# A decoder layer's weight products: one load per block for two sums, reordered branch loads, and accumulating transfers in the output projection

## Chip, cores, metric

One core of one Trainium2 chip. The metric is device time of one execution in microseconds (us). TensorE's granted clock is one of two levels, 1.2 and 2.4 GHz; the profile shows it as 0.5 and 1.

## What is computed

One decoder layer on 512 tokens of width 2048, in float32. Cut to what matters:

```
proj = rms_norm(x) @ w_in                      # 2048 x 14928
y_a, y_b, y_m = three branches of proj, each 512 x 1024
merged = sigmoid(g_a) * (y_a @ w_branch_a) + sigmoid(g_b) * (y_b @ w_branch_b)
       + sigmoid(g_m) * (y_m @ w_branch_m)     # w_branch_*: 1024 x 2048
out = x + merged @ w_out                       # 2048 x 2048
```

Branch a is a gated MLP: a layer norm over v, a causal mix inside each chunk of 128 tokens, then a product with gelu(u) and silu(z).

## The kernel before

**Every product is three.** A float32 operand is split into a high and a low part: ScalarE (ACT) casts the high part and VectorE (DVE) subtracts it from the source (`split`, L136 and L137). `three` (L160 to L162) multiplies high by high, low by high and high by low. Weights pass through in blocks of 128 x 2 x 512 floats (512 KB, "one pair" of k tiles). The tile `raw` has four slots, the split parts `whi` and `wlo` three each. One pair in a block product is 12 matmuls.

**Strassen units.** Eight units of 1024 columns (v, z, m, m, b, b, a, a) of `w_in` go through `strassen` (L836): each needs seven block products instead of eight, A11, S1, S2, A12, S3, A22, N4, each of four pairs (48 matmuls). The weight operand of a product is either a block as loaded (`passing`, into `raw`) or a running sum of blocks kept in SBUF, `va` (tile `a`) and `vb` (tile `b`), to which DVE adds the next block (L847). S1 reads `va`, then adds block (1,1) to it (`b11_12`, L865); S2 reads `va`, loads block (1,1) again and adds it to `vb` (`b11_12_22`, L871); A12 reads block (1,0) as loaded and adds it to `va` (L877). `kept_as` stores each result to DRAM from the POOL (GpSimd) queue.

**The last unit** also starts loads for what follows, all from the POOL queue, as `last_unit` (L948) places them: after S1 the operand `ym` of branch m (four loads of 1 MB), after S3 `after_s3` (L935: a gate block, the factors of chunk 0, the layer norm's gain and bias), after A22 the operand `yb` of branch b (four of 1 MB).

**Branch stage** (L1078): for m, b, a and each of four column groups a product of 96 matmuls, whose result DVE multiplies by the gate (L1095) and adds up (L1097). `gating` (L963), a generator, does branch a's MLP for four chunks between the products; `pump` runs it a few steps per k tile against a credit, and each `yield` names what the step takes. Its input tiles come by `factors_load` (L928). `finish(made)` runs what is left of it before branch a's first product.

**Output projection**: `output_unit` (L1114) twice, 1024 columns of `w_out` each, in the order A11, S3, S1, S2, A12, A22, N4. All weight loads and the stores to `out` are issued on the SP (SyncE) queue, in one order; the blocks of `x` come into one tile, `score`, from POOL (`x_part`, L1127), and DVE adds them. The first of the two units runs while DVE still prepares its operands (`right_half`, `parts_of`).

**Order.** The build orders each engine's instructions by what it takes to be ready, not by the place in the code alone: an instruction can stand ahead of others that the code has earlier. On the chip each engine and queue then keeps that order.

Of the kernel before, what the change touches and what calls it, by code (L numbers as in the profile page):

```python
# [17 lines left out]
P = 128  # L18
# [41 lines left out]
def hybrid_block(ctx: ExitStack, tc: tile.TileContext, a, out):  # L60
# [41 lines left out]
    def submit(gen):  # L102
        tasks.append(gen)
        return gen
# [716 lines left out]

    pairs = range(0, 8, CK)

    def block_product(op, ps, operand, onto=False, budget=None):
        ah, al = op
        for k in pairs:
# [9 lines left out]
    def strassen(w, c0, finished, placing=None, after={}):  # L836
# [12 lines left out]
        def product(name, *args, **k):  # L849
            block_product(ops[name], *args, **k)  # L850
            if name in after:
                after[name]()

        va, vb = {}, {}

        def b11(k):
            va[k] = load(held("a"), 0, 0, k)
            parts = split_pair(va[k])
            vb[k] = load(held("b"), 0, 1, k)
            add(va[k], vb[k])  # L860
            if k == 8 - CK and placing:
                placing()
            return parts

        def b11_12(k):  # L865
            c = passing(1, 1, k)
            parts = split_pair(va[k])
            add(va[k], c)
            return parts

        def b11_12_22(k):  # L871
            c = passing(1, 1, k)
            parts = split_pair(va[k])
            add(vb[k], c)
            return parts

        def b21(k):  # L877
            c = passing(1, 0, k)
            parts = split_pair(c)
            add(va[k], c)  # L880
            return parts

        x = bank()
        product("A11", x, b11)
# [12 lines left out]
        x = bank()  # L897
        e3 = ev()
        V.tensor_tensor(e3, z, e1, op=OP.subtract)
        finished(1, 512, e3)  # L900
        product("A22", x, lambda k: split_pair(va[k]))
        V.tensor_tensor(e1, x, e1, op=OP.add)
        finished(1, 0, e1)
        product("N4", z, lambda k: split_pair(passing(1, 1, k)), onto=True)
        V.tensor_tensor(e2, z, e2, op=OP.subtract)
        finished(0, 512, e2)

    def kept_as(kept, func):
        def finished(th, col, t, psum=None):
# [6 lines left out]
    y_of, sgs, uvz, lnp = {}, {}, {}, []  # L916

    def y_load(name):
        y_of[name] = tuple(big16(f"y{name}{n}") for n in range(2))
        for n in range(2):  # L920
            for f in (0, 4):
                G.dma_start(y_of[name][n][:, f:f + 4, :].bitcast(F32), y_kept[name][n, :, f:f + 4, :])

    def gate_load(name, cg):
        sgs[name, cg] = big8([P, 4, T])
# [6 lines left out]

    wide8 = lambda: (big8([P, 2, 1024]), big8([P, 2, 1024]))

    def after_s3():  # L935
        gate_load("m", 0)
        factors_load(0, wide8)
        lnp.append(big8([P, 2, 1024]))
        for i, name in enumerate(("gain", "bias")):
            G.dma_start(lnp[0][:, i, :], a["gmlp_ln_" + name].partition_broadcast(P))  # L940
# [17 lines left out]
    y_of["a"] = tuple(pools["cpool"].tile([P, 8, T], F32R, tag=f"ya{n}", name=f"ya{n}") for n in range(2))  # L958
    odd8 = lambda tag="odd1": pools["cpool"].tile([P, 2, 1024], F32, tag=tag, name=tag)
    odd_two = lambda: (odd8("odd0"), odd8("odd1"))  # L960
    factors_load(1, odd_two)

    def gating():  # L963
        for c in range(NT):
            vo, uz = uvz.pop(c)
            u, v, o = uz[:, 0, :], vo[:, 0, :], vo[:, 1, :]
            bs = tiny.tile([P, 2, 6], F32, name="bn_s")
# [25 lines left out]
            for g2 in range(2):  # L993
# [84 lines left out]
    for name, cg in [(name, cg) for first in (0, 2) for name in "mba" for cg in (first, first + 1)]:  # L1078
        if (name, cg) not in sgs:
            gate_load(name, cg)  # L1080
        if name == "a" and made in tasks:
            finish(made)
        sg = sgs.pop((name, cg))
        ah, al = y_of[name]
        ps = [bank(), bank()]
        for k, hi, lo in chunks(a["w_branch_" + name], cg * 512, 512, 8):
# [24 lines left out]
    stage = opened(("ev", 4), ("hold", 4))  # L1111
    w_out = a["w_out"]

    def output_unit(c0, first):  # L1114
        wv = w_out.rearrange("(k p) c -> p k c", p=P)

        def load(to, kh, ch, k):
            SP.dma_start(to, wv[:, kh * 8 + k:kh * 8 + k + CK, c0 + ch * 512:c0 + ch * 512 + 512])
# [5 lines left out]
        def add(to, x):  # L1124
            V.tensor_tensor(to, to, x, op=OP.add)

        def x_part(th, col):  # L1127
            xr = score_all[:, :1024].rearrange("p (t c) -> p t c", c=512)
            G.dma_start(xr, a["x"].rearrange("(t p) c -> p t c", p=P)[:, 2 * th:2 * th + 2, c0 + col:c0 + col + 512])  # L1129
            return xr  # L1130

        def store(th, col, t, ts=slice(0, 2)):
            SP.dma_start(out.rearrange("(t p) c -> p t c", p=P)[:, 2 * th:2 * th + 2, c0 + col:c0 + col + 512][:, ts],
                         t[:, ts])
# [12 lines left out]

        def b11_12_22(k):
            add(va[k], passing(1, 1, k))
            return split_pair(va[k])  # L1150

        def b21(k):
            c = passing(1, 0, k)
            parts = split_pair(c)
            add(va[k], c)
            return parts

        bud = 1300 if first else None
# [6 lines left out]
        if first:  # L1165
            finish(submit(parts_of("S2")))
            n4_made = submit(parts_of("N4"))
# [5 lines left out]
        if first:  # L1173
            finish(n4_made)
        add_to = lambda o, p, q, op: V.tensor_tensor(o, p, q, op=op)  # L1175
        add_to(e1, y, e1, OP.add)
        e3 = ev()
        add_to(e3, z, e1, OP.subtract)
        add_to(e7, e1, e7, OP.subtract)
        xr = x_part(0, 0)  # L1180
        block_product(gops["A12"], x, b21, onto=True)
        add_to(xr, x, xr, OP.add)
        store(0, 0, xr)
        xr = x_part(1, 512)
        add_to(e3, e3, xr, OP.add)
        store(1, 512, e3)
        xr = x_part(1, 0)
        x = bank()
        add_to(xr, xr, e1, OP.add)
        block_product(gops["A22"], x, lambda k: split_pair(va[k]))  # L1190
        add_to(xr, x, xr, OP.add)
        store(1, 0, xr)
        xr = x_part(0, 512)
        add_to(e7, e7, xr, OP.subtract)
        block_product(gops["N4"], z, lambda k: split_pair(passing(1, 1, k)), onto=True)
        for t in range(2):
            add_to(e7[:, t], z[:, t], e7[:, t], OP.subtract)
            store(0, 512, e7, slice(t, t + 1))
# [41 lines left out]
```

## Time and profile before

| | us |
|---|---|
| median of 3 runs (1862.53 to 1866.06) | 1864.43 |
| the profiled execution, its own time | 1864.7 |
| its span, first to last instruction | 1863.0 |
| PE (TensorE) busy in it | 1811.2 |
| DVE busy | 1261.0 |
| ACT busy | 760.6 |

A row of the waits or of the timeline names the engine, the line, the operation and its tiles; "idle before <-X" says what ended the idle time. POOL and SP issue transfers. In the table of stretches each row is a stretch of the span, with busy time and instruction count of each engine, then the granted clock, the DMA engines' busy share and their rate.

### The profile page before, as it was taken

The numbers are of one execution on the slowest core, as the hardware profiler recorded it, in microseconds if no ns is written. First come the engines' busy times: TensorE is split into PE (matmuls) and PEld (weight loads), VectorE is DVE, ScalarE is ACT, GpSimd is POOL, SyncE is SP. The second block draws the span as 40 slices with busy tenths as digits, with TensorE's granted clock in tenths as the row PEclk, the third lists the DMA queues.
The fourth block names the chain that finished last, engine by engine and source line by source line (L and its number), as shares of the span: only waits on it lengthen the run. The fifth ranks groups of instructions, "written<-read, shape, count | busy, mean of one in ns | idle before, by whom it ended". The sixth has DMA issues, their size and how long they took to land. (4 is left out here: it accounts for less than half of the span.)

```text
span 1863.0 us, 21854 instructions
## 1 busy us (share of the span) xinstructions
PE 1811.2 (97%) x8426; PEld 1512.3 (81%) x8426; DVE 1261.0 (68%) x1667; ACT 760.6 (41%) x986; POOL 95.1 (5%) x155
## 2 busy tenths in 40 slices
PE   8999999999999999999999999999897999998997
PEld 6798899888888888888888888888786888886776
DVE  7787679665436466968678687786755543559685
ACT  4754442353334354444444444444351222225332
POOL 7000000000000000000000000000010000000000
PEclk9999999999999999999999999999998999998999
DMA  7744223333332424675665755756765544337673
GB/s 231 276 127 119 77 81 87 113 114 113 91 102 60 135 68 142 223 220 162 187 209 181 214 181 181 219 165 213 260 245 196 193 135 136 114 119 275 213 228 124
DMA packets 141720, 304.03 MB, mean 163 GB/s; under 512 B 10032, under 2 KB 16176, under 8 KB 139568
## 3 DMA queue, kind: packets, MB, share of 16 engines
q1 hardware_dynamic: 127200, 242.39, 41.9%
q0 software_dynamic: 14128, 60.23, 8.9%
q8 instruction: 66, 1.08, 0.2%
q14 instruction: 38, 0.31, 0.1%
q10 hardware_dynamic: 288, 0.02, 0.0%
HBM read 271.14 MB, written 31.46 MB: 162 GB/s over the span
## 5 line engine op out<-in xcount | busy, mean ns | idle before, releaser
L137 DVE TENSOR_TENSOR wlo<-raw,whi 128x1024 fp32r<-128x1024 f32 (+1 forms) x280 | 339.8, 1216 | 299.4 <-ACT whi L136 299.0
L136 ACT CAST whi<-raw 128x1024 fp32r<-128x1024 f32 (+1 forms) x280 | 288.5, 1031 | 566.3 <-PE xyz L162 275.8
L136 ACT CAST whi<-a 128x1024 fp32r<-128x1024 f32 x152 | 160.0, 1054 | 211.5 <-PE xyz L162 195.1
L161 PE MATMUL xyz<-wlo,hTh 128*128 128x512 f32 x576 | 225.2, 391 | 6.5 <-DVE wlo L137 6.5
L160 PE MATMUL xyz<-whi,hTh 128*128 128x512 f32 x576 | 224.9, 390 | 0.7 <-ACT b L752 0.7
L162 PE MATMUL xyz<-whi,hTl 128*128 128x512 f32 x576 | 225.0, 391 | 0.0
L137 DVE TENSOR_TENSOR wlo<-a,whi 128x1024 fp32r<-128x1024 f32 x152 | 184.7, 1221 | 48.8 <-ACT whi L136 48.3
L160 PE MATMUL acc<-whi,hTh 128*128 128x512 f32 (+1 forms) x544 | 203.5, 374 | 0.3 <-ACT b L639 0.3
L161 PE MATMUL acc<-wlo,hTh 128*128 128x512 f32 (+1 forms) x544 | 200.9, 369 | 0.0
L162 PE MATMUL acc<-whi,hTl 128*128 128x512 f32 (+1 forms) x544 | 200.6, 369 | 0.0
L161 PEld LDWEIGHTS xyz<-wlo,hTh 128*128 128x128 f32 x576 | 108.7, 189 | 29.6 <-DVE wlo L137 7.0
L160 PEld LDWEIGHTS xyz<-whi,hTh 128*128 128x128 f32 x576 | 108.7, 189 | 23.7 <-ACT b L752 1.1
L162 PEld LDWEIGHTS xyz<-whi,hTl 128*128 128x128 f32 x576 | 108.7, 189 | 22.6
L160 PEld LDWEIGHTS acc<-whi,hTh 128*128 128x128 f32 x544 | 102.2, 188 | 13.5 <-ACT b L639 0.7
L162 PEld LDWEIGHTS acc<-whi,hTl 128*128 128x128 f32 x544 | 102.1, 188 | 13.5
L161 PEld LDWEIGHTS acc<-wlo,hTh 128*128 128x128 f32 x544 | 102.3, 188 | 11.9
L185 PE MATMUL acc<-hTh,whi 128*128 128x512 f32 x256 | 100.1, 391 | 0.0
L186 PE MATMUL acc<-hTl,whi 128*128 128x512 f32 x256 | 99.7, 390 | 0.0
L187 PE MATMUL acc<-hTh,wlo 128*128 128x512 f32 x256 | 99.7, 389 | 0.0
L847 DVE TENSOR_TENSOR a<-a,raw 128x1024 f32<-128x1024 f32 x64 | 76.9, 1221 | 9.2 <-DMA raw<-w_in 8.7
L137 DVE TENSOR_TENSOR wlo<-b,whi 128x1024 fp32r<-128x1024 f32 x40 | 49.0, 1224 | 47.7 <-ACT whi L136 47.7
L136 ACT CAST whi<-b 128x1024 fp32r<-128x1024 f32 x40 | 42.0, 1050 | 47.0 <-PE xyz L162 42.2
(357 smaller groups left out, 3542.3 us busy)
## 6 DMA issues: line engine op xcount, KB each, us to landing
raw<-w_in SPq DMA_DIRECT2D x216, 512.0 KB, 3.6
raw<-w_out SPq DMA_DIRECT2D x48, 512.0 KB, 4.4
a<-w_in SPq DMA_DIRECT2D x32, 512.0 KB, 4.5
b<-w_in SPq DMA_DIRECT2D x32, 512.0 KB, 3.8
raw<-w_mem_kv SPq DMA_DIRECT2D x31, 512.0 KB, 4.7
raw<-w_in SPq DMA_DIRECT2D x24, 368.0 KB, 3.1
raw<-w_branch_m SPq DMA_DIRECT2D x16, 512.0 KB, 5.1
raw<-w_branch_b SPq DMA_DIRECT2D x16, 512.0 KB, 3.7
```

Source lines behind the costliest of these rows:

```text
L136: S.copy(hi, src)
L137: V.tensor_tensor(lo, src, hi.bitcast(F32), op=OP.subtract)
L160: PE.matmul(ps, lhsT=lh, rhs=rh, start=first, stop=False, **k)
L161: PE.matmul(ps, lhsT=lh, rhs=rl, start=False, stop=False, **k)
L162: PE.matmul(ps, lhsT=ll, rhs=rh, start=False, stop=last, **k)
L185: PE.matmul(ps[i][:m], lhsT=hi[:, f:f + m], rhs=ah[:, k, :], start=(k == 0), stop=False)
L186: PE.matmul(ps[i][:m], lhsT=hi[:, f:f + m], rhs=al[:, k, :], start=False, stop=False)
L187: PE.matmul(ps[i][:m], lhsT=lo[:, f:f + m], rhs=ah[:, k, :], start=False, stop=(k == ktiles - 1))
L847: V.tensor_tensor(to, to, x, op=OP.add)
```

## The change

1. `strassen`: block (1,1) is loaded once, in S1, and DVE adds it there to `va` and to `vb`; S2 neither loads nor adds.
2. `block_product` takes a list of calls and makes one after each pair. In the last unit the four loads of `ym` are asked for after S2's second and fourth pair and A12's first and second; the gate block, gain and bias, and chunk 0's factors after A22's first, second and third. `yb` is loaded at the start of branch m's second product. Chunk 1's and 3's factors are loaded inside `gating`, chunk 2's after chunk 1, with larger yields.
3. Output projection: `output_unit` is replaced by `first_output_unit` and, for the second half, by `strassen` with the same operands. In the first, the sums of S3 and S1 are made by a transfer from POOL that adds into the tile (`accum_op`) in place of a load and a DVE add. In both, `x` is added to three of four result blocks by such a transfer and they are stored from POOL; the last has `x` subtracted by DVE before N4, and is stored from SP.

```diff
         def product(name, *args, **k):
-            block_product(ops[name], *args, **k)
-            if name in after:
-                after[name]()
+            block_product(ops[name], *args, after=after.get(name, ()), **k)
...
         def b11_12(k):
             c = passing(1, 1, k)
             parts = split_pair(va[k])
             add(va[k], c)
+            add(vb[k], c)
             return parts
 
         def b11_12_22(k):
-            c = passing(1, 1, k)
-            parts = split_pair(va[k])
-            add(vb[k], c)
-            return parts
+            return split_pair(va[k])
...
+        if before_last:
+            before_last(e2)
         product("N4", z, lambda k: split_pair(passing(1, 1, k)), onto=True)
-        V.tensor_tensor(e2, z, e2, op=OP.subtract)
-        finished(0, 512, e2)
+        for t in (slice(0, 1), slice(1, 2)) if before_last else (slice(0, 2),):
+            V.tensor_tensor(e2[:, t], z[:, t], e2[:, t], op=OP.subtract)
+            finished(0, 512, e2, ts=t)
...
-    last_unit = {"S1": lambda: y_load("m"), "S3": after_s3, "A22": lambda: y_load("b")}
+    last_unit["S2"] = [lambda: None, first_of(ym), lambda: None, first_of(ym)]
+    last_unit["A22"] = [lambda: gate_load("m", 0), norm_load, lambda: factors_load(0, wide8)]
...
-    factors_load(1, odd_two)
...
         for c in range(NT):
+            if c + 1 < NT and c % 2 == 0:
+                factors_load(c + 1, odd_two)
...
-            if c + 2 < NT:
-                factors_load(c + 2, odd_two if c else wide8)
-                yield 3000
+            if c == 1:
+                factors_load(2, wide8)
+                yield 9000
+            elif c == 0:
+                yield 6000
...
+        if name == "m" and cg == 1:
+            for load in y_load("b"):
+                load()
...
+    def given_out(c0):
+        def finished(th, col, t, psum=None, ts=None):
+            o = ev() if t is None else t
+            if psum is not None:
+                S.copy(o, psum)
+            if ts is None:
+                G.dma_start(o, tiles_of(a["x"], th, c0 + col), accum_op=OP.add)
+                G.dma_start(tiles_of(out, th, c0 + col), o)
+            else:
+                SP.dma_start(tiles_of(out, th, c0 + col)[:, ts], o[:, ts])
+        return finished
+
+    def less_x(c0):
+        xr = score_all[:, :1024].rearrange("p (t c) -> p t c", c=512)
+        G.dma_start(xr, tiles_of(a["x"], 0, c0 + 512))
+        return lambda e2: V.tensor_tensor(e2, e2, xr, op=OP.subtract)
...
         def b12_22(k):
             vb[k] = load(held("b"), 0, 1, k)
-            add(vb[k], passing(1, 1, k))
+            G.dma_start(vb[k], block(1, 1, k), accum_op=OP.add)
             return split_pair(vb[k])
 
         def b11_12(k):
             va[k] = load(held("a"), 0, 0, k)
-            add(va[k], passing(0, 1, k))
+            G.dma_start(va[k], block(0, 1, k), accum_op=OP.add)
             return split_pair(va[k])
...
+        less = less_x(0)
         block_product(gops["A12"], x, b21, onto=True)
-        add_to(xr, x, xr, OP.add)
-        store(0, 0, xr)
+        finished(0, 0, None, x)
...
-    output_unit(0, True)
-    output_unit(1024, False)
+    first_output_unit()
+    strassen(w_out, 1024, given_out(1024), ops=gops, before_last=less_x(1024))
```

## Rows read from the trace of the kernel before

**Rows 1.** The page's part 1: busy time, share of the span, instructions.

```profile
PE 1811.2 (97%) x8426; PEld 1512.3 (81%) x8426; DVE 1261.0 (68%) x1667; ACT 760.6 (41%) x986; POOL 95.1 (5%) x155
```

**Rows 2.** Waits of PE: who, for what, us in total, times, longest.

```profile
PE xyz L161 <- DVE wlo L137: 18.0, 8, 6.5
PE xyz L160 <- DVE b L1095: 7.4, 2, 6.6
PE xyz L160 <- ACT whi L136: 5.5, 1, 5.5
```

**Rows 3.** Table of stretches, last unit of `w_in`: S2, then A12.

```profile
1319.60:1330.50 10.90, 10.90 (x50) 9.03 (x49) 8.40 (x8) 4.22 (x4) 2.15 (x4) 1.00 0.97 359
1330.50:1350.50 20.00, 13.47 (x50) 10.60 (x49) 10.66 (x11) 4.21 (x4) 1.29 (x2) 0.83 0.77 288
```

**Rows 4.** Timeline of POOL and DVE in the same two products.

```profile
1320.05 2.15 POOL L922 DMA_DIRECT2D ym<-y_m  x4 [17.69 <-PE xyz L162]
...
1337.92 1.23 DVE L847 TENSOR_TENSOR a<-a,raw 128x1024 f32<-128x1024 f32 x1 [4.05 <-DMA raw<-w_in]
```

**Rows 5.** Timeline of DVE and PE, start of S1 in the unit before the last.

```profile
1152.62 1.22 DVE L137 TENSOR_TENSOR wlo<-a,whi 128x1024 fp32r<-128x1024 f32 x1
...
1159.71 2.36 DVE L137 TENSOR_TENSOR wlo<-a,whi 128x1024 fp32r<-128x1024 f32 x2
...
1156.84 0.39 PE L161 MATMUL xyz<-wlo,hTh 128*128 128x512 f32 x1
```

**Rows 6.** Table of stretches, branch stage: first and second product of branch m.

```profile
1383.20:1405.50 22.30, 22.22 (x99) 18.03 (x97) 4.81 (x4) 6.34 (x6) 3.63 (x6) 1.00 0.93 335
1405.50:1443.80 38.30, 28.21 (x121) 22.59 (x120) 24.43 (x43) 6.50 (x9) 1.82 (x3) 0.82 0.48 166
```

**Rows 7.** Timeline of DVE and POOL in the branch stage.

```profile
1407.47 0.69 DVE L970 BATCH_NORM_STATS2 bn_s<-odd 128x6 f32<-128x512 f32 x1 [11.43 <-DMA odd<-kept_v]
...
1416.61 1.22 DVE L1095 TENSOR_TENSOR b<-b,xyz 128x1024 f32<-128x1024 f32 x1
...
1550.47 0.75 POOL L926 DMA_DIRECT2D b<-kept_b  x1 [2.02 <-PE aux L1014]
```

**Rows 8.** Table of stretches, output projection: first unit's S3, S1, N4; second's A11, S3; the end.

```profile
1690.00:1711.40 21.40, 14.39 (x49) 11.12 (x49) 20.80 (x20) 10.24 (x10) 0.71 (x1) 0.76 0.80 283
1711.40:1722.90 11.50, 11.13 (x49) 8.92 (x48) 11.32 (x11) 5.97 (x6) 0.00 (x0) 1.00 0.97 349
...
1755.60:1773.90 18.30, 13.73 (x49) 10.47 (x48) 9.35 (x8) 4.20 (x4) 1.43 (x2) 0.85 0.67 233
1773.90:1786.30 12.40, 11.88 (x50) 9.43 (x49) 9.02 (x9) 4.20 (x4) 0.71 (x1) 0.94 0.72 215
1786.30:1798.40 12.10, 11.10 (x49) 8.90 (x48) 10.29 (x10) 5.12 (x5) 0.00 (x0) 1.00 0.91 315
...
1853.40:1863.00 9.60, 0.03 (x1) 0.00 (x0) 2.51 (x3) 0.00 (x0) 0.25 (x1) 0.70 0.32 109
```

**Rows 9.** Timeline of DVE and SP, first output unit's S3.

```profile
1693.35 1.22 DVE L1125 TENSOR_TENSOR b<-b,raw 128x1024 f32<-128x1024 f32 x1
...
1683.60 2.27 SPq L1118 DMA_DIRECT2D b<-w_out  x4
1687.78 0.37 SPq L1118 DMA_DIRECT2D a<-w_out  x1
```

**Rows 10.** DMA issues: tile, queue, count, KB of one, median us to landing.

```profile
b<-kept_m POOLq DMA_DIRECT2D x4, 1024.0 KB, 8.7
...
score<-x POOLq DMA_DIRECT2D x8, 512.0 KB, 5.6
```

**Rows 11.** Timeline of DVE: first unit's N4, and the end of the kernel.

```profile
1765.30 1.23 DVE L1175 TENSOR_TENSOR score<-score,ev 128x1024 f32<-128x1024 f32 x1 [5.12 <-DMA score<-x]
...
1857.17 1.23 DVE L1175 TENSOR_TENSOR ev<-ev,score 128x1024 f32<-128x1024 f32 x1 [6.59 <-DMA score<-x]
1858.50 1.29 DVE L1175 TENSOR_TENSOR ev<-xyz,ev 128x512 f32<-128x512 f32 x2
```

More of the change, by code (lines that the diff above doesn't have):

```diff
@@ L822, in hybrid_block, with block_product @@
     pairs = range(0, 8, CK)
-    def block_product(op, ps, operand, onto=False, budget=None):
+    def block_product(op, ps, operand, onto=False, budget=None, after=()):
         ah, al = op
+        after = iter(after)
         for k in pairs:
@@ L834, in block_product, with strassen @@
                 pump(budget)
-    def strassen(w, c0, finished, placing=None, after={}):
+            next(after, lambda: None)()
+        for rest in after:
+            rest()
+    def strassen(w, c0, finished, placing=None, after={}, ops=ops, before_last=None):
         wv = w.rearrange("(k p) c -> p k c", p=P)
@@ L903, in strassen @@
         finished(1, 0, e1)
+        if before_last:
+            before_last(e2)
         product("N4", z, lambda k: split_pair(passing(1, 1, k)), onto=True)
-        V.tensor_tensor(e2, z, e2, op=OP.subtract)
-        finished(0, 512, e2)
+        for t in (slice(0, 1), slice(1, 2)) if before_last else (slice(0, 2),):
+            V.tensor_tensor(e2[:, t], z[:, t], e2[:, t], op=OP.subtract)
+            finished(0, 512, e2, ts=t)
     def kept_as(kept, func):
-        def finished(th, col, t, psum=None):
+        def finished(th, col, t, psum=None, ts=None):
             o = ev() if t is None else t
@@ L919, in y_load, with part @@
         y_of[name] = tuple(big16(f"y{name}{n}") for n in range(2))
-        for n in range(2):
-            for f in (0, 4):
-                G.dma_start(y_of[name][n][:, f:f + 4, :].bitcast(F32), y_kept[name][n, :, f:f + 4, :])
+        def part(n, f):
+            G.dma_start(y_of[name][n][:, f:f + 4, :].bitcast(F32), y_kept[name][n, :, f:f + 4, :])
+        return [lambda n=n, f=f: part(n, f) for f in (0, 4) for n in range(2)]
     def gate_load(name, cg):
@@ L933, in hybrid_block, with norm_load @@
     wide8 = lambda: (big8([P, 2, 1024]), big8([P, 2, 1024]))
-    def after_s3():
-        gate_load("m", 0)
-        factors_load(0, wide8)
+    def norm_load():
         lnp.append(big8([P, 2, 1024]))
@@ L947, in hybrid_block, with ym_loads @@
     SP.dma_start(sb, a["spatial_b"])
-    last_unit = {"S1": lambda: y_load("m"), "S3": after_s3, "A22": lambda: y_load("b")}
+    last_unit = {}
+    def ym_loads():
+        loads = y_load("m")
+        last_unit["A12"] = loads[2:]
+        for load in loads[:2]:
+            load()
+            yield
+    ym = ym_loads()
+    first_of = lambda gen: lambda: next(gen, None)
+    last_unit["S2"] = [lambda: None, first_of(ym), lambda: None, first_of(ym)]
+    last_unit["A22"] = [lambda: gate_load("m", 0), norm_load, lambda: factors_load(0, wide8)]
     for name, c0, n, func in (("v", O_AV, 1024, AF.Gelu_apprx_tanh), ("z", O_AZ, 1024, AF.Silu),
@@ L1083, in hybrid_block @@
         sg = sgs.pop((name, cg))
+        if name == "m" and cg == 1:
+            for load in y_load("b"):
+                load()
         ah, al = y_of[name]
@@ L1112, in hybrid_block, with finished, first_output_unit @@
     w_out = a["w_out"]
-    def output_unit(c0, first):
+    tiles_of = lambda t, th, c: t.rearrange("(t p) c -> p t c", p=P)[:, 2 * th:2 * th + 2, c:c + 512]
+    def given_out(c0):
+        def finished(th, col, t, psum=None, ts=None):
+            o = ev() if t is None else t
[11 more added lines that the diff above has]
+        return lambda e2: V.tensor_tensor(e2, e2, xr, op=OP.subtract)
+    def first_output_unit():
         wv = w_out.rearrange("(k p) c -> p k c", p=P)
+        block = lambda kh, ch, k: wv[:, kh * 8 + k:kh * 8 + k + CK, ch * 512:ch * 512 + 512]
         def load(to, kh, ch, k):
-            SP.dma_start(to, wv[:, kh * 8 + k:kh * 8 + k + CK, c0 + ch * 512:c0 + ch * 512 + 512])
+            SP.dma_start(to, block(kh, ch, k))
             return to
@@ L1122, in passing @@
             return load(wpool.tile([P, CK, 512], F32, tag="raw", name="raw", bufs=4), kh, ch, k)
[L1124 to L1134, printed above, removed]
         va, vb = {}, {}
@@ L1144, in b11_12 @@
             va[k] = load(held("a"), 0, 0, k)
-            add(va[k], passing(0, 1, k))
+            G.dma_start(va[k], block(0, 1, k), accum_op=OP.add)
             return split_pair(va[k])
         def b11_12_22(k):
-            add(va[k], passing(1, 1, k))
+            V.tensor_tensor(va[k], va[k], passing(1, 1, k), op=OP.add)
             return split_pair(va[k])
@@ L1154, in b21 @@
             parts = split_pair(c)
-            add(va[k], c)
+            V.tensor_tensor(va[k], va[k], c, op=OP.add)
             return parts
-        bud = 1300 if first else None
+        finished = given_out(0)
+        bud = 1300
         x = bank()
@@ L1164, in output_unit @@
         block_product(gops["S3"], y, b12_22, budget=bud)
-        if first:
-            finish(submit(parts_of("S2")))
-            n4_made = submit(parts_of("N4"))
+        finish(submit(parts_of("S2")))
+        n4_made = submit(parts_of("N4"))
         e7 = ev()
@@ L1172, in output_unit @@
         block_product(gops["S2"], y, b11_12_22, onto=True, budget=bud)
[L1173 to L1176, printed above, removed]
+        finish(n4_made)
+        V.tensor_tensor(e1, y, e1, op=OP.add)
         e3 = ev()
-        add_to(e3, z, e1, OP.subtract)
-        add_to(e7, e1, e7, OP.subtract)
-        xr = x_part(0, 0)
+        V.tensor_tensor(e3, z, e1, op=OP.subtract)
+        finished(1, 512, e3)
+        V.tensor_tensor(e7, e1, e7, op=OP.subtract)
+        less = less_x(0)
         block_product(gops["A12"], x, b21, onto=True)
-        add_to(xr, x, xr, OP.add)
-        store(0, 0, xr)
[L1184 to L1187, printed above, removed]
+        finished(0, 0, None, x)
         x = bank()
-        add_to(xr, xr, e1, OP.add)
         block_product(gops["A22"], x, lambda k: split_pair(va[k]))
[L1191 to L1194, printed above, removed]
+        V.tensor_tensor(e1, x, e1, op=OP.add)
+        finished(1, 0, e1)
+        less(e7)
         block_product(gops["N4"], z, lambda k: split_pair(passing(1, 1, k)), onto=True)
-        for t in range(2):
-            add_to(e7[:, t], z[:, t], e7[:, t], OP.subtract)
-            store(0, 512, e7, slice(t, t + 1))
+        V.tensor_tensor(e7, z, e7, op=OP.subtract)
+        finished(0, 512, e7, ts=slice(0, 2))
     halves = submit(right_half(1, *(quad(ev()) for _ in range(3))))
-    output_unit(0, True)
-    output_unit(1024, False)
+    first_output_unit()
+    strassen(w_out, 1024, given_out(1024), ops=gops, before_last=less_x(1024))
     stage.close()
```

## The prediction, made before the change was run

> **What bounds the kernel now.** I read the page's busy times first: PE is busy for 97% of the span, DVE for 68% [rows 1]. So the kernel is a row of matmuls, and only time in which PE waits, or runs slowly after a wait, can be won. PE's waits come to 18.0, 7.4 and 5.5 us [rows 2], 31 us in all: for a low part that DVE makes, for a result bank that DVE empties, for a high part from ACT. The table of stretches then shows where they lie and what they cost with the slow clock behind them. A block product with nothing in its way takes 10.9 us, the last unit's S2 for one [rows 3], so 2.72 us for each of its four pairs; what a product takes beyond that is its loss.
>
> - Last unit of w_in, A12: 20.0 us, a loss of 9.1; the granted clock averages 0.83 there [rows 3], part of it at the lower level, 1.2 GHz.
> - Second product of branch m: 38.3 us against 22.3 for the first [rows 6], 16.0 more, some of it gating's own small matmuls.
> - First output unit: S3 21.4, a loss of 10.5, S1 11.5, a loss of 0.6; N4 18.3, and then the second unit's A11 12.4 and S3 12.1, a loss of 10.1 together [rows 8].
> - After PE's last matmul: 9.6 us [rows 8].
>
> **The change, part by part**, against the profiled execution's own 1864.7 us, which is 0.3 above the median of the three runs.
>
> *One load for two sums, in the last unit.* POOL issues the four loads of ym together at 1320.05, when S1 lets go of their space, and the DMA engines are then busy for 0.97 of S2. A12's own weights are asked for in the same stretch, and DVE still waits for one at 1337.92 [rows 3, 4]. They are late because four slots of raw must first pass S1's four blocks and then the same four again for S2. After the change the slots turn over once less: A12's blocks take the slots that S1's sums give back, all during S1, so before the ym loads or beside their first. Next in need would be N4's blocks, two products later. I take the whole 9.1.
>
> *Dealing out the loads.* I expect nothing from it. The load of the kept_b gate for the fourth column group leaves at 1550.47 [rows 7], although the code asks for it at that product's start, two products of about 22 us and part of a third later: a POOL load leaves when its space is free, not where the code has it. The space of ym comes free at S1's end and that of yb at A22's end, before and after. If they do leave later, the first case already has the gain, so the term is 0 here.
>
> *The sums move from S2 to S1, in all eight units and in the second output unit.* DVE then has three operations per pair in S1. Two in a row take 2.36 us, so one costs 1.14; three are 3.4 against PE's 2.72, 0.7 short per pair, 2.8 per product. The cover is DVE's lead: S1's first low part is done at 1153.84 and used at 1156.84 [rows 5], 3.0 us. S2 has one operation per pair left and restores it. So between 0 and, without any lead, 2.8 x 8 = 22.4; the lead row is nearest, and I take 1 us over all units for a late block. Without the 16 MB of second loads nothing else gets faster, since no product there waits for DMA.
>
> *Branch stage.* DVE reaches chunk 1's statistics before the low part that PE needs and stands 11.43 us until v has landed; the emptying of the first product's banks follows only at 1416.61 [rows 7]. v waits for the space that the last unit's stores leave, and those wait behind yb and the branch weights (0.93 busy [rows 6]). The change asks for v inside gating, but its space decides, as above. The slot that chunk 2's v used to take now goes to a gate block of twice the size, which can put chunk 1 later; chunk 2's own statistics move behind the emptying, which can put that earlier. Between 5.6 lost (one more landing of 512 KB [rows 10]) and the 16.0 gained: I take 0, since what ends the wait is the same.
>
> *Yields.* Before branch a's first product pump gives 24 x 1900 = 45,600; the first three chunks now cost 46,800, so all of chunk 3 falls to finish(made), where before only its end did. PE can run the other chunks' matmuls meanwhile. Between 0 and four DVE operations of 1.22 us in a chain (4.9): I take 1.
>
> *Sums of S3 and S1 by transfers.* S3 of the first output unit ought to start at 1690.0; DVE, busy 20.8 of 21.4 us with right_half and these sums, comes to the first of them at 1693.35 [rows 8, 9]. Eight sums, 9.1 us of DVE, go. In their place POOL waits for each block, adds the second by a transfer, and behind it in POOL's queue stand the next sums, the x block and the stores. No row shows an accumulating transfer; the nearest is the 512 KB load from POOL, 5.6 us, and beyond it the 1 MB one, 8.7 [rows 10]. The first block is asked for at 1683.60 [rows 9] at the latest, and earlier by some us as two raw loads ahead of it go: 1683.6 + 5.6 + 0.7 (POOL's issue, as in the 0.75 of [rows 7]) + 5.6 + 2.3 for the two parts is 1697.8, hardly better than now; with the loads 5 us earlier it is 1692.8. For S1 the first block's space is free at 1687.78 [rows 9]; by the same sum its parts stand at 1702.0, against a start at 1700.9 or later. The gain lies between 11.1 (all of it) and a loss: if the eight sums move twice the bytes, 4.2 MB more at the 349 GB/s that S1's stretch already moves at 0.97 busy [rows 8] are 12 us. I take a gain of 3, near the plain load's row.
>
> The Trainium skill, page "Collectives: The Full Stack", section "The bandwidth ceiling: the fold count and why AG ≠ RS ≠ AR", says that an adding transfer needs two source reads and so runs at about half a copy's rate. By it this term would be the loss and not the gain; it is the second rival below. No run here shows one yet.
>
> *x by transfers.* DVE's waits for x, as at 1765.30 [rows 11], hold the low parts behind them, and SP's stores hold N4's loads. Both leave these queues: the result waits for DVE or ACT, then for POOL, and what is queued behind it on POOL is only the next result. ACT's one more copy lies in its idle time (4.2 busy of 18.3 [rows 8]). The first unit's last store stays on SP, and the next unit's loads may stand behind it. Of 10.1 I take 9.5.
>
> *The end.* DVE waits 6.59 for the last x block and starts the last subtraction at 1858.50, 5.1 after PE's end at 1853.4 [rows 8, 11]. With x taken off before N4 it starts at once. Late next is the result before it: DVE, an adding transfer, a store, about 1.2 + 0.7 + 5.6 + 5.6 after A22, while N4 and the last stores take longer. I take 4.5.
>
> Sum: 1864.7 - 9.1 + 1 + 0 + 1 - 3 - 9.5 - 4.5 = 1840.6; set off by the 0.3, 1840.3 for the median.
>
> **Rivals.**
> - *Adding transfers cost double.* For it: S1's stretch is nearly full already. Against: DVE has no part in them. The gain of 3 becomes a loss of 9: 1852.3.
> - *The branch stage's wait goes as well.* For it: the order of DVE's work there hangs on a few us, and chunk 2 leaves it. Against: the same stores still end the wait. Some 12 of 16: 1828.
> - *The last unit's wait stays*: the change would not do what it says, if A12's blocks still stood behind ym. Against: the slots turn over once less. 1849.4.
> - *DVE falls short in S1.* Full price 22.4 in place of 1: 1861.7, no change. Against: the 3.0 of lead.
> - *Slower: the adding transfers run one behind the other, each holding the path for t.* Place: S1 of the first output unit. Its last sum would have its parts at 1683.6 + 5.6 + 8t + 2.3, and is needed at 1700.9 + 8.2: a wait of 8t - 17.6. The rest wins 21.1, and the loss that S3 and S1 have now, 11.1, is in it too; so it decides from t = 6.2, more than a plain load's whole time to landing. At t = 8 the time is 1879. Against: the four loads of b leave within 2.27 us [rows 9] and run side by side.
>
> **How the numbers follow.** Chances: forecast 0.52; double cost 0.18; branch stage too 0.14; last unit's wait stays 0.06; DVE short 0.04; serial transfers 0.06. About 0.2%, 3.7 us, is what a measurement can tell from no change: faster 0.52 + 0.18 + 0.14 + 0.06 = 0.90, same 0.04, slower 0.06. The range goes from 1827, the branch stage's case, to 1857, the double cost with 5 for the other unknown terms; the last two cases, 0.10, stay out, and a tail of the others.
>
> **What would show it.** A12 of the last unit in 10.9 us with ym still leaving in one burst; the second product of m still some 14 over; S1 in the w_in units at 10.9 each; in the first output unit S3 some 7 over, N4 at 10.9; the last store about 4 us after PE. It is wrong if adding transfers land later than some 9 us after their issue, or if PE waits for low parts in S1.

## The result, and the profile after

The changed kernel takes 1846.06 us (median of 4 runs, 1845.57 to 1846.42); the kernel before took 1863.48 in the same comparison. The ratio is 0.9905, 95% interval 0.9887 to 0.9922: about 17.4 us faster. The forecast was 1840.3, range 1827 to 1857. The profiled execution took 1846.4 us against 1864.7, so there are 18.3 us to be found in the profile.

Part 1 of the page of the changed kernel answers to [rows 1], and the waits of PE on the same three operations to [rows 2]. DVE has lost 16.4 us of work, POOL has gained 18.9, and the wait for DVE's low parts has gone from 18.0 to 4.5 us. The wait for a high part from ACT has grown from 5.5 to 12.2.

```profile
PE 1804.9 (98%) x8426; PEld 1508.2 (82%) x8426; DVE 1244.6 (67%) x1652; ACT 762.2 (41%) x987; POOL 114.0 (6%) x169
```

```profile
PE xyz L160 <- ACT whi L136: 12.2, 2, 10.4
PE xyz L160 <- DVE b L1119: 6.9, 2, 6.4
...
PE xyz L161 <- DVE wlo L137: 4.5, 6, 2.2
```

The table of stretches of the changed kernel, cut at the same products as [rows 3, 6, 8]: S2 and A12 of the last unit of `w_in`; the two products of branch m; S3 and S1 of the first output unit; its N4, then A11 and S3 of the second; and what follows PE's last matmul.

```profile
1320.00:1330.90 10.90, 10.90 (x50) 9.03 (x49) 9.92 (x9) 4.22 (x4) 2.15 (x4) 1.00 0.97 377
1330.90:1341.80 10.90, 10.90 (x49) 9.03 (x49) 6.04 (x5) 4.22 (x4) 1.81 (x3) 1.00 1.01 380
1374.40:1396.70 22.30, 22.23 (x99) 18.07 (x97) 4.81 (x4) 6.45 (x6) 4.41 (x7) 1.00 0.96 366
1396.70:1431.60 34.90, 26.35 (x119) 21.72 (x120) 21.86 (x37) 6.51 (x9) 1.58 (x3) 0.85 0.50 170
1677.50:1706.00 28.50, 14.83 (x50) 10.44 (x49) 12.74 (x12) 10.04 (x10) 10.10 (x9) 0.76 1.08 284
1706.00:1720.10 14.10, 13.18 (x48) 10.21 (x49) 11.14 (x10) 6.05 (x6) 0.00 (x0) 0.88 0.87 227
1753.00:1763.60 10.60, 10.60 (x48) 8.80 (x47) 7.59 (x7) 4.20 (x4) 1.97 (x2) 1.00 0.97 303
1763.60:1774.70 11.10, 11.10 (x50) 9.19 (x50) 11.10 (x11) 4.23 (x4) 0.74 (x1) 1.00 0.38 131
1774.70:1785.40 10.70, 10.70 (x48) 8.85 (x48) 10.70 (x10) 5.13 (x5) 0.00 (x0) 1.00 0.48 160
1840.00:1844.70 4.70, 0.00 (x0) 0.00 (x0) 1.29 (x2) 0.00 (x0) 0.00 (x0) 0.92 0.29 112
```

Read the length of each stretch (the second number) against its partner of before:

| stretch | before | after | difference | forecast |
|---|---|---|---|---|
| A12, last unit | 20.0 | 10.9 | -9.1 | -9.1 |
| second product of m | 38.3 | 34.9 | -3.4 | 0 |
| S3 and S1, first output unit | 32.9 | 42.6 | **+9.7** | **-3** |
| N4, then A11 and S3 of the second unit | 42.8 | 32.4 | -10.4 | -9.5 |
| after PE's last matmul | 9.6 | 4.7 | -4.9 | -4.5 |
| sum | | | -18.1 | -26.1 |

(The forecast's two terms of +1, for S1 in the units of `w_in` and for the yields, have no stretch of their own.) The rows hold 18.1 of the 18.3 us. Four of the five stretches went as forecast or better; S3 and S1, whose sums are now made by adding transfers, went the other way. Where S3 and S1 lose it is seen in POOL's queue and in ACT, which makes the high part of each sum as soon as it has landed (POOL's timeline, then ACT's, of the changed kernel):

```profile
1677.14 3.76 POOL L1174 DMA_DIRECT2D b<-w_out  x3 [52.27 <-DMA b<-w_out]
1681.18 1.19 POOL L1174 DMA_DIRECT2D b<-w_out  x1 [0.28 <-issue]
1684.51 0.74 POOL L1155 DMA_DIRECT2D score<-x  x1 [2.14 <-DVE gN4l L137]
1685.23 2.48 POOL L1179 DMA_DIRECT2D a<-w_out  x2
1690.13 1.21 POOL L1179 DMA_DIRECT2D a<-w_out  x1 [2.42 <-DMA a<-w_out]
1694.07 1.19 POOL L1179 DMA_DIRECT2D a<-w_out  x1 [2.73 <-DMA a<-w_out]
```

```profile
1686.94 1.04 ACT L136 CAST whi<-b 128x1024 fp32r<-128x1024 f32 x1 [5.27 <-DMA b<-w_out]
...
1690.99 1.05 ACT L136 CAST whi<-b 128x1024 fp32r<-128x1024 f32 x1 [2.06 <-DMA b<-w_out]
1694.95 1.05 ACT L136 CAST whi<-b 128x1024 fp32r<-128x1024 f32 x1 [2.91 <-DMA b<-w_out]
1699.07 1.05 ACT L136 CAST whi<-b 128x1024 fp32r<-128x1024 f32 x1 [3.08 <-DMA b<-w_out]
1704.90 1.04 ACT L136 CAST whi<-a 128x1024 fp32r<-128x1024 f32 x1 [4.78 <-DMA a<-w_out]
```

The four adding transfers of S3 are issued within 5.2 us (1677.14 to 1682.37), but the first sum is there 9.8 us after its issue and the others 4.0 us apart. S1's first sum, issued at 1685.23 behind them and the x block, is there 19.7 us later. PE's timeline shows what each costs: the first matmul of S3 waits 10.43 us (5.5 before, the wait for ACT in [rows 2]), and S1 starts 1.78 late. Of the 4.5 us of waits for `wlo`, 2.24 stand in branch m, at 1398.88, and the other five waits, 2.30 together, in S3 and S1 of the first output unit: there is none left for S1 in the units of `w_in`.

```profile
1398.88 0.50 PE L161 MATMUL xyz<-wlo,ym 128*128 128x512 f32 x1 [2.24 <-DVE wlo L137]
...
1406.69 0.79 PE L160 MATMUL xyz<-whi,ym 128*128 128x512 f32 x1 [6.37 <-DVE b L1119]
...
1688.04 0.79 PE L160 MATMUL xyz<-whi,S 128*128 128x512 f32 x1 [10.43 <-ACT whi L136]
...
1706.00 0.51 PE L160 MATMUL xyz<-whi,gS1h 128*128 128x512 f32 x1 [1.78 <-ACT whi L136]
```

In the branch stage DVE still waits for v, 9.27 us in place of 11.43 [rows 7], and begins to empty the first product's banks 8.4 us after that wait's end (9.1 before):

```profile
1397.00 0.69 DVE L989 BATCH_NORM_STATS2 bn_s<-odd 128x6 f32<-128x512 f32 x1 [9.27 <-DMA odd<-kept_v]
...
1405.42 2.35 DVE L1119 TENSOR_TENSOR b<-b,xyz 128x1024 f32<-128x1024 f32 x2
```

### The profile page after: what moved, and what is told of

Its sections match the earlier page's. It is cut to its first block, busy times and chain, and to the rows that moved or that the text cites. A ratio compares the mean times of both kernels' runs of the same rounds, so it can differ in the third digit from the quotient of the medians.

```text
span 1844.7 us, 21738 instructions
## 1 busy us (share of the span) xinstructions
PE 1804.9 (98%) x8426; PEld 1508.2 (82%) x8426; DVE 1244.6 (67%) x1652; ACT 762.2 (41%) x987; POOL 114.0 (6%) x169
## 3 DMA queue, kind: packets, MB, share of 16 engines
q8 instruction: 66, 1.08, 0.2%
## 4 chain that ended last, share of the span: by engine, by line
issue 52%; PE 37%; DMA 5%; DVE 3%; POOL 2%; ACT 1%; SPq 0%; DVEq 0%; POOLq 0%; ACTq 0%
PE xyz L160 6%; PE xyz L161 6%; PE xyz L162 6%; PE acc L161 3%; PE acc L162 3%; PE acc L160 3%; DMA a<-w_out 2%; PE acc L185 1%; PE acc L186 1%; PE acc L187 1%; DVE wlo L137 1%; DMA raw<-w_branch_m 1%; DVE mTl L256 0%; PE aux L514 0%; PE aux L513 0%
## 5 line engine op out<-in xcount | busy, mean ns | idle before, releaser
L137 DVE TENSOR_TENSOR wlo<-raw,whi 128x1024 fp32r<-128x1024 f32 (+1 forms) x276 | 333.7, 1210 | 315.0 <-ACT whi L136 314.7
L136 ACT CAST whi<-raw 128x1024 fp32r<-128x1024 f32 (+1 forms) x276 | 284.2, 1031 | 556.3 <-PE xyz L162 275.7
L136 ACT CAST whi<-a 128x1024 fp32r<-128x1024 f32 x156 | 164.4, 1055 | 221.3 <-PE xyz L162 205.2
L852 DVE TENSOR_TENSOR a<-a,raw 128x1024 f32<-128x1024 f32 x72 | 86.4, 1220 | 0.4
```

Source lines behind the costliest of these rows:

```text
L136: S.copy(hi, src)
L137: V.tensor_tensor(lo, src, hi.bitcast(F32), op=OP.subtract)
```

## The experiments

"S3 and S1" below is the sum of the two stretches of the first output unit; 21.8 would be no loss.

### The first two parts, each alone

**e1_one_load**: the kernel before with the first part of the change alone.

```diff
             add(va[k], c)
+            add(vb[k], c)
             return parts
...
         def b11_12_22(k):
-            c = passing(1, 1, k)
-            parts = split_pair(va[k])
-            add(vb[k], c)
-            return parts
+            return split_pair(va[k])
```

> The kernel before with part 1 alone: block (1,1) loaded once in S1 and added to both sums there. Theory (A12's blocks come a turn of the raw slots earlier): A12 of the last unit falls from 20.0 to 10.9 us, the time from 1863.5 to about 1854.4. Rival (the dealing out makes that gain): A12 stays at 20.0, the time at 1863.5. Rival (DVE falls short in S1): PE waits for low parts in S1 or S2 of all eight units, up to 2.8 us each, 1854.4 plus up to 22.

Measured: 1853.31 us, ratio 0.9945 (0.9930 to 0.9960), against 1864.28 of before on the same chip: 11.0 less, the theory's figure within 1.1. A12 of the last unit in the table of stretches:

```profile
1330.60:1341.40 10.80, 10.80 (x49) 8.97 (x48) 4.96 (x5) 4.22 (x4) 1.29 (x2) 1.00 1.00 369
```

**e2_dealt**: the kernel before with the second part alone (the loads of `ym`, the gate block, the factors and `yb` dealt out).

```diff
-    last_unit = {"S1": lambda: y_load("m"), "S3": after_s3, "A22": lambda: y_load("b")}
...
+    last_unit["S2"] = [lambda: None, first_of(ym), lambda: None, first_of(ym)]
+    last_unit["A22"] = [lambda: gate_load("m", 0), norm_load, lambda: factors_load(0, wide8)]
```

> The kernel before with part 2 alone: the last unit's loads dealt out, yb, the factors and the yields moved; two loads of block (1,1) and the old output units. Theory (POOL's loads leave when their space is free, not at their place in the code): the four loads of ym still leave together at S1's end, A12 stays at 20.0 us; the second product of m may lose 3 us less, as in the changed kernel: 1860.5 to 1863.5. Rival (dealing out thins the burst): A12 near 10.9 and 1854 or less.

Measured: 1862.36 (10 runs, 1858.0 to 1863.77), ratio 0.9986 (0.9977 to 0.9996), as the theory had it. A12 is as slow as before and still waits for its own blocks:

```profile
1330.00:1351.00 21.00, 13.84 (x49) 10.92 (x48) 9.44 (x8) 4.19 (x4) 1.82 (x3) 0.76 0.80 306
```

```profile
1337.84 1.23 DVE L852 TENSOR_TENSOR a<-a,raw 128x1024 f32<-128x1024 f32 x1 [3.62 <-DMA raw<-w_in]
```

So the wait of A12 goes with the one load, wholly, and dealing out does nothing for it. In the changed kernel the four loads of `ym` also still leave in one burst. What differs is the place of A12's own blocks, seen in SP's queue (the kernel before, then the changed one; from 1316 to 1323), and below them the burst of the changed kernel:

```profile
1316.68 6.05 SPq L840 DMA_DIRECT2D raw<-w_in  x4
```

```profile
1316.15 2.64 SPq L845 DMA_DIRECT2D raw<-w_in  x2
```

```profile
1320.32 2.15 POOL L927 DMA_DIRECT2D ym<-y_m  x4 [17.97 <-PE xyz L162]
```

Before, A12's last two blocks got their slots from DVE's additions for S2, at 1321.22 and 1322.36, behind the start of the burst at 1320.05 [rows 4]; they landed at 1332.56 and 1337.83, with DVE waiting for each. In the changed kernel its last two leave at 1316.15 and 1318.42, ahead of the burst, and have landed by 1321.83. S2's own last block had landed at 1321.18 before, so it is the turn of the slots, and not the bytes of the second loads, that put A12's last two blocks behind `ym`.

**e8_undealt**: the changed kernel with all sums by DVE (e3_sums_dve, below) and the second part undone, the other way round.

```diff
-    last_unit["S2"] = [lambda: None, first_of(ym), lambda: None, first_of(ym)]
-    last_unit["A22"] = [lambda: gate_load("m", 0), norm_load, lambda: factors_load(0, wide8)]
+    last_unit = {"S1": [lambda: None] * 4 + [lambda: y_load("m")], "S3": [lambda: None] * 4 + [after_s3], "A22": [lambda: None] * 4 + [lambda: y_load("b")]}
...
+    factors_load(1, odd_two)
```

> The changed kernel with all eight sums on DVE (1835.0) and part 2 undone: the last unit's loads, yb, the factors and the yields as before. Theory (part 2 is worth only the 2 to 4 us that the second product of m loses less): 1837 to 1839, A12 of the last unit still 10.9. Rival (with one load the dealing out keeps the burst from A12): 1840 or more, and A12 waits.

Measured: 1840.36 (1838.15 to 1841.07) against 1835.01 of e3_sums_dve (1833.15 to 1837.25), 5.3 more; the two profiled executions are only 2.8 apart. That is above the theory's 1837 to 1839, but A12 has no loss, so the rival is out. The second product of m takes 36.3:

```profile
1330.80:1341.70 10.90, 10.90 (x49) 9.03 (x49) 4.81 (x4) 4.21 (x4) 1.29 (x2) 1.00 1.00 383
1397.00:1433.30 36.30, 26.04 (x119) 21.50 (x120) 24.99 (x43) 6.50 (x9) 1.81 (x3) 0.86 0.49 172
```

Across the kernels this product takes 38.3, 37.7 and 36.3 us without the second part (before, e1_one_load, e8_undealt) and 34.9, 33.2 and 35.3 with it (the changed kernel, e2_dealt, e3_sums_dve). The second part as a whole is worth some 2 to 5 us: 1.9 by the medians of e2_dealt and before, 5.3 by those of e8_undealt and e3_sums_dve. The product itself is 5.1 shorter in the profiles of the first pair, where that of e2_dealt is one of its fastest executions, and 1.0 in those of the second; the rest of the second difference has no place that the profiles show.

### The sums of S3 and S1

**e3_sums_dve**: the changed kernel with all eight sums made as before, by a load and an addition on DVE.

```diff
-            G.dma_start(vb[k], block(1, 1, k), accum_op=OP.add)
+            V.tensor_tensor(vb[k], vb[k], passing(1, 1, k), op=OP.add)
...
-            G.dma_start(va[k], block(0, 1, k), accum_op=OP.add)
+            V.tensor_tensor(va[k], va[k], passing(0, 1, k), op=OP.add)
```

> The changed kernel with the sums of S3 and S1 in the first output unit by a load and a DVE add again; x still by adding transfers. Theory (the adding transfers are what S3 and S1 wait for): the loss of S3, S1 and S2 falls from 20.3 to about the 11.1 of the kernel before, 1846.1 becomes 1837. Rival (the stretch is short of DMA whichever way the sums are made): within 2 us of 1846.

Measured: 1835.01, ratio 0.9846 (0.9832 to 0.9861): 11.0 below the changed kernel, 2 below the theory's figure. S3 and S1 take 31.8:

```profile
1677.20:1697.20 20.00, 13.02 (x49) 10.24 (x49) 20.00 (x18) 10.17 (x10) 0.71 (x1) 0.83 0.83 291
1697.20:1709.00 11.80, 11.13 (x49) 8.90 (x48) 11.80 (x12) 5.96 (x6) 0.00 (x0) 1.00 0.98 353
```

**e4_plain**: the changed kernel with the same eight transfers in the same queue, but plain: the additions of these blocks are left out.

```diff
-            G.dma_start(vb[k], block(1, 1, k), accum_op=OP.add)
+            G.dma_start(vb[k], block(1, 1, k))
...
-            G.dma_start(va[k], block(0, 1, k), accum_op=OP.add)
+            G.dma_start(va[k], block(0, 1, k))
```

> The changed kernel with the eight transfers for the sums of S3 and S1 as plain loads over the first block, from the same queue, in the same order and with the same waits; the additions of these blocks are left out. Theory (the adding itself takes the DMA engines about twice as long): their landings, 4.0 us apart in the changed kernel, come to 3.0 apart or less, S3 and S1 lose 5 to 9 us less, 1837 to 1841. Rival (the two queues take turns and the add is free): still 4.0 apart, 1846.

Measured: 1834.75, ratio 0.9843 (0.9827 to 0.9860). S3 and S1 take 32.8, and the high parts follow each other 1.9 us apart:

```profile
1675.60:1697.60 22.00, 13.84 (x50) 10.72 (x49) 16.70 (x15) 11.10 (x11) 6.14 (x9) 0.77 1.03 409
1697.60:1708.40 10.80, 10.80 (x49) 8.97 (x48) 9.52 (x9) 5.13 (x5) 0.00 (x0) 1.00 0.72 262
```

```profile
1682.39 1.04 ACT L136 CAST whi<-b 128x1024 fp32r<-128x1024 f32 x1 [2.50 <-DMA b<-w_out]
...
1684.29 1.04 ACT L136 CAST whi<-b 128x1024 fp32r<-128x1024 f32 x1
1686.22 1.04 ACT L136 CAST whi<-b 128x1024 fp32r<-128x1024 f32 x1 [0.90 <-DMA b<-w_out]
```

The issues of S3's four, first in the changed kernel and then here (KB of one, median us to landing):

```profile
b<-w_out POOLq DMA_DIRECT2D x4, 512.0 KB, 14.0
```

```profile
b<-w_out POOLq DMA_DIRECT2D x4, 512.0 KB, 8.0
```

This isolates the price of adding: the queue, the order and the bytes of the blocks are the same, and 11.3 us of the total go with the addition, more than the theory's 5 to 9. The DMA engines are full in both (1.08 with the sums and 1.03 plain; the share adds up the times of packets, which overlap, so it can pass 1), but the stretch of S3 moves 409 GB/s plain and 284 with the sums: the adding transfers take more of the engines for what they carry. The ratio of the two distances, 4.0 and 1.9 us, is 2.1, but it is not the price by itself, because loads of S1's first blocks from SP land between: in the changed kernel one for each sum (at 1689.43 and 1693.46; POOL goes on behind them, at 1690.13 and 1694.07), here one for every two of POOL's (at 1682.83 and 1686.46). An estimate from these rows: three plain loads in 3.8 us are 1.3 each, and 4.0 less 1.3 leaves 2.7 for a sum, again 2.1 times.

The Trainium skill ("Collectives: The Full Stack", section "The bandwidth ceiling: the fold count and why AG ≠ RS ≠ AR") says of the adding step of a collective that it needs two source reads, and puts ReduceScatter at about half the rate of AllGather, which copies. Carried over to these transfers, as an estimate, that is a price of 2, and the trace agrees with its 2.1.

The run shows a second thing: even transfers that add nothing bring S3 no further than DVE's additions did, since they take 8.0 us to landing behind the first block's own load. The 11.1 us that the forecast held for the most that could be won there were not to be had by this route, whatever adding costs.

**e5_s1_only** and **e6_s3_only**: adding transfers in one place, DVE in the other.

```diff
 # e5_s1_only
-            G.dma_start(vb[k], block(1, 1, k), accum_op=OP.add)
+            V.tensor_tensor(vb[k], vb[k], passing(1, 1, k), op=OP.add)
```

```diff
 # e6_s3_only
-            G.dma_start(va[k], block(0, 1, k), accum_op=OP.add)
+            V.tensor_tensor(va[k], va[k], passing(0, 1, k), op=OP.add)
```

> The changed kernel with S3's sums by a load and a DVE add and S1's still by adding transfers. Theory (four adding transfers 4.0 us apart fit ahead of S1, eight do not fit ahead of S3 and S1): S1 waits for nothing, S3 loses about 9 as with all sums on DVE, 1831 to 1836. Rival (any adding transfer there makes PE wait): 1839 or more.

> The changed kernel with S3's sums by adding transfers and S1's sums by a load and a DVE add. Theory (S3 pays: its blocks are needed one product after they are asked for, and adding transfers land some 4 us apart there, while S1's have a product more of time): S3 loses 14 us or more, the total 1840 to 1847. Rival (what costs is the eight adding transfers following each other on one queue, so that four of them in either place cost little): within 2 us of 1835, S3 losing 9 to 11.

Measured: e5_s1_only 1834.47, ratio 0.9836 (0.9821 to 0.9851); e6_s3_only 1840.60, ratio 0.9875 (0.9859 to 0.9892). S3 and S1 take 32.1 and 38.4:

```profile
1675.20:1696.50 21.30, 14.29 (x49) 11.08 (x49) 19.73 (x18) 11.28 (x11) 5.59 (x5) 0.76 1.05 307
1696.50:1707.30 10.80, 10.80 (x49) 8.96 (x48) 8.16 (x8) 5.12 (x5) 0.00 (x0) 1.00 1.06 356
```

```profile
1675.50:1702.20 26.70, 14.07 (x50) 10.31 (x49) 16.61 (x15) 11.07 (x11) 5.55 (x5) 0.74 0.98 271
1702.20:1713.90 11.70, 11.31 (x49) 8.79 (x48) 11.60 (x11) 5.13 (x5) 0.00 (x0) 1.00 0.92 309
```

Both came out as their theories had it. Over e3_sums_dve, S3's four cost 5.6 us, S1's four nothing, and all eight 11.0. So the price is not the number of transfers: S3 needs its sums at once and pays for them, while S1 has a product's time to wait for its own. S1 loses that time when S3's four come first; S3 then takes 28.5 and not 26.7, and S1 14.1 and not 11.7. Whether S1's sums wait there for their place in the queue or for the engines, which both sets share, no run parts.

### Two smaller questions

**e7_odd_first**: does v's space hold it in the branch stage? e3_sums_dve with chunk 1's tiles taken first from their pool and their loads asked for there.

```diff
-    y_of["a"] = tuple(pools["cpool"].tile([P, 8, T], F32R, tag=f"ya{n}", name=f"ya{n}") for n in range(2))
...
+    factors_load(1, odd_two)
+    y_of["a"] = tuple(pools["cpool"].tile([P, 8, T], F32R, tag=f"ya{n}", name=f"ya{n}") for n in range(2))
...
-            if c + 1 < NT and c % 2 == 0:
+            if c == 2:
```

> The changed kernel with all eight sums on DVE (1835.0), and the tiles of chunk 1's factors placed first in the new pool, on the space of the last unit's weight sums, where they stood on the space of its result tiles. Theory (chunk 1's v waits for the last unit's stores, DVE for v, PE for DVE): v leaves before the last store, the second product of m loses 3 us or less where it lost 11.4, 1825 to 1828. Rival (v is late because the DMA engines are full): no more than 2 us from 1835.

Measured: 1833.43 (1832.27 to 1834.72), 1.6 below e3_sums_dve with overlapping runs: the rival's figure, not the theory's 1825 to 1828. v leaves at 1383.73, 10.1 us after the start of m's first product (16.5 in e3_sums_dve), and DVE still waits 7.76 for it:

```profile
1383.73 0.55 POOL L938 DMA_DIRECT2D odd<-kept_v  x1 [0.41 <-DMA raw<-w_branch_m]
```

```profile
1393.66 0.69 DVE L990 BATCH_NORM_STATS2 bn_s<-odd 128x6 f32<-128x512 f32 x1 [7.76 <-DMA odd<-kept_v]
```

Issued 6.3 us sooner in its stage, it lands 1.7 us sooner: 9.9 us to landing in place of 5.3, with the last load of `yb` and the branch weights under way and the DMA engines 1.03 busy from 1383.7 to 1393.7. In e8_undealt the code asks for v as early, but on the old space, and v leaves 17.9 us after the product's start. So space decides when the load leaves, as the prediction said, but not alone when it arrives.

**e9_pool_stores**: is it SP's stores that hold the first output unit's N4? e1_one_load with the output stores issued from POOL.

```diff
-            SP.dma_start(out.rearrange("(t p) c -> p t c", p=P)[:, 2 * th:2 * th + 2, c0 + col:c0 + col + 512][:, ts],
+            G.dma_start(out.rearrange("(t p) c -> p t c", p=P)[:, 2 * th:2 * th + 2, c0 + col:c0 + col + 512][:, ts],
```

> The kernel before with one load for two sums (1853.3) and the output units' stores issued from POOL in place of SP; x still comes by plain loads into one tile and is added by DVE. Theory (N4 of the first unit loses its 7 us because DVE stands waiting for x ahead of the low parts): the loss stays, 1851 to 1855. Rival (N4's weight loads stand behind stores in SP's queue): N4 at 10.9, about 1846.

Measured: 1859.37, ratio 0.9968 (0.9955 to 0.9981): 4 us (by the ratios) to 6 us (by the medians) slower than e1_one_load, and above the theory's 1851 to 1855. N4 takes 19.6, and DVE waits for x:

```profile
1747.90:1767.50 19.60, 14.48 (x49) 10.99 (x48) 9.26 (x8) 4.16 (x4) 2.15 (x3) 0.83 0.55 175
```

```profile
1750.66 1.23 DVE L1173 TENSOR_TENSOR ev<-ev,score 128x1024 f32<-128x1024 f32 x1 [5.94 <-DMA score<-x]
...
1760.83 1.23 DVE L1173 TENSOR_TENSOR score<-score,ev 128x1024 f32<-128x1024 f32 x1 [6.67 <-DMA score<-x]
```

So N4's loss does not need stores on SP: without them there it loses as much, to x. The rival's 10.9 is out. How much the stores took before is not shown, since here they stand ahead of x in POOL's queue: DVE's two waits for x are 5.94 and 6.67 us, where they were 4.75 and 5.10 in e1_one_load.

**e10_both_best**: the edits of e5_s1_only and e7_odd_first together.

```diff
-            G.dma_start(vb[k], block(1, 1, k), accum_op=OP.add)
+            V.tensor_tensor(vb[k], vb[k], passing(1, 1, k), op=OP.add)
...
-    y_of["a"] = tuple(pools["cpool"].tile([P, 8, T], F32R, tag=f"ya{n}", name=f"ya{n}") for n in range(2))
...
+    factors_load(1, odd_two)
+    y_of["a"] = tuple(pools["cpool"].tile([P, 8, T], F32R, tag=f"ya{n}", name=f"ya{n}") for n in range(2))
...
-            if c + 1 < NT and c % 2 == 0:
+            if c == 2:
```

> The changed kernel with S3's sums by a load and a DVE add, S1's sums by adding transfers, and chunk 1's factor tiles placed first (the edits of e5_s1_only and e7_odd_first together). Theory (the two touch different stages, so the gains add): 1831 to 1834 us. Rival (each was worth less than the spread of its runs, so nothing adds): 1833.5 to 1836.

Measured: 1834.53, ratio 0.9838 (0.9824 to 0.9853): the rival's figure, nothing adds. m's second product, 32.2 in the profile of e7_odd_first, takes 35.0 here with the same order of work:

```profile
1395.80:1430.80 35.00, 27.41 (x119) 22.50 (x120) 21.19 (x37) 6.52 (x9) 1.57 (x3) 0.85 0.46 162
```

Here v leaves 4.8 us sooner in its stage than in e3_sums_dve and lands 0.3 sooner. So no run shows that e7_odd_first's gain is more than the spread. e3_sums_dve, e5_s1_only, e7_odd_first and e10_both_best can't be told apart, and each beats both kernels: their intervals end at 0.9861 or below, that of the change begins at 0.9887. The simplest of them is the change with its eight sums given back to DVE.

## Why the prediction was right, and where it was not

- **One load for two sums, -9.1**: right in size and cause, -9.1 in its stretch and 11.0 alone in e1_one_load. As the prediction said, A12's blocks now leave ahead of `ym`, and the wait went although `ym` left in one burst.
- **Dealing out, 0**: right that the loads of `ym` don't move and that A12 gains nothing. The 2 to 5 us that the second part is worth were not in any term; what of them the profiles show is in the branch stage.
- **Sums from S2 to S1, +1**: PE waits nowhere in S1 of the units of `w_in`; the lead covered it. The rival "DVE falls short in S1" is out. (Its full price counts eight units; with the second output unit, which the term names too, 2.8 x 9 would be 25.2.)
- **Branch stage, 0**: -3.4; the wait is still ended by v, as forecast, but it is shorter. Of the 2.4 us by which the banks are emptied sooner after the start of m's first product, 1.7 are v's earlier landing and 0.7 the shorter way from there. That way is 9.1 us in all three kernels without the second part, with two statistics of chunk 2 on DVE in it, and 8.4 in all five with it, without them: this is the move that the prediction named as what can put it earlier. The other 1.0 us of the stretch is not placed.
- **Yields, +1**: no wait of PE stands there; from the end of m's second product to S3 of the first output unit it is 246.2 us before and 245.9 after. About 0.
- **x by transfers, -9.5, and the end, -4.5**: -10.4 and -4.9. Of the two causes named for the first, DVE's waits for x hold; what SP's stores took is not shown (e9_pool_stores). The transfers were not put back by themselves in the changed kernel; what stands for the term are the rows of the stretches, and e1_one_load, which keeps the old x and N4's loss with it. A sum of runs on one chip agrees: e3_sums_dve is 29.3 us below before, e1_one_load 11.0 and e2_dealt 1.9, so, if the parts add, 16.4 are left for x and the end, where the stretches have 15.3.
- **Sums of S3 and S1 by transfers, -3**: the step that failed; it came to +9.7. The sum took 5.6 us to landing, "near the plain load's row", for an adding transfer, and let four of them run side by side because the plain loads of b do. Two things were wrong in it. Plain transfers already take 8.0 us to landing there and win 0.1 in these stretches, not 3 (e4_plain, 32.8 against 32.9). Adding then puts 9.8 on top: S3's four land 9.8 to 17.8 us after their issue and 4.0 apart. By the prediction's own sign (adding transfers that land later than some 9 us after their issue) it was wrong here. The rival "adding transfers cost double", called the second and listed first, had this term at +9, with the right mechanism (e4_plain). Its time, 1852.3, was 6 too high only because the other terms together came out 6.7 better than forecast.
- **The rival "slower"** had another part of it: the sums do come one behind the other, and S1's lose when S3's go first (e5_s1_only). At its formula's 8t - 17.6, with the 4.0 us of the trace for t, S1 would wait 14.4; S3 and S1 lost 20.8 in all, since the formula left out S3's own wait. As 4.0 is below the 6.2 from which that rival decides, the change was still a gain.

The total came within 6 us of the forecast by luck: two errors, -6.7 and +12.7, partly cancelled, and the rival with the right mechanism for the sums missed by as much on the other side. The sign was safe: the parts that were read from waits with a plain owner (a slot that turns over twice, an x block that arrives late) held to a microsecond.

## What to carry to other kernels

A transfer that adds is no free addition: on a stretch whose DMA engines are full it took the place of about two plain ones here, so use it where the sum is not needed for a product's length, as for x here, and leave the addition to DVE where the next product waits for it. Ahead of moving work off a busy engine, ask whether the next product would start sooner with that work gone: e4_plain, which left the additions out, was no faster than DVE doing them. And to find why a load is late, look for what turns its buffer over: one load fewer per pair was worth more here than a new order of all the loads behind it.

## What the runs showed of the hardware that was not expected

- An adding transfer of 512 KB takes longer even when the DMA engines are not full. In the last 45 us of the changed kernel (DMA share 0.41) the three for x took 6.1 us to landing, where the three plain loads of x in the last 45 us of the kernel before (0.37) took 4.2 (the DMA issues of the two stretches; KB of one, then median us):

```profile
ev<-x POOLq DMA_DIRECT2D x3, 512.0 KB, 6.1
```

```profile
score<-x POOLq DMA_DIRECT2D x3, 512.0 KB, 4.2
```

- It also holds POOL longer at its issue: 1.19 us against the 0.74 of a plain one, in the rows of POOL shown first (1681.18 and 1684.51).
- On full DMA engines an earlier issue buys little: v, issued 6.3 us sooner in its stage, landed 1.7 us sooner (e7_odd_first against e3_sums_dve), and issued 4.8 sooner, 0.3 sooner (e10_both_best).
